# Three places for the rests of a masked sum, each behind one place of the block cycle, and idle matmuls counted by place

## The chip, the cores and the metric

The kernel runs on one core of a Trainium2 chip. The metric is the device time in microseconds (us). A core has engines that run side by side: TensorE (PE, matrix products), VectorE (DVE), ScalarE (ACT), GpSimd (POOL) and SyncE (SP, which here only issues transfers). Transfers between the main memory and the on-chip memory are done by 16 DMA engines, which take work from the queues of SP and ACT.

## What is computed

For each of 8 sequences, `x` is masked past `lengths`, summed cumulatively, and the sum at the midpoint is taken and multiplied with `w`:

```python
B, S, D = 8, 8192, 512
masked = x * (pos < lengths)
cs = np.cumsum(masked, axis=1)
mid_features = cs[b_idx, lengths // 2, :]
return np.matmul(mid_features[:, None, :], w).squeeze(1)
```

Only the first n = min(lengths // 2 + 1, lengths) rows of each sequence are needed, so each row of the result is the sum of n rows of `x`, times `w`. For the lengths drawn here n is 570, 2690, 256, 2057, 905, 3772, 3859 and 571: 30.1 MB of `x` of the 134 MB.

## The kernel before

Each sequence's n rows are cut into full blocks of 512 rows (1 MB, spread as 128 partitions x 4 rows) and a rest of fewer than 512 rows. Rows are summed by PE: a matmul with a one-hot column of weights (128 x 8) adds 128 rows into the row of the right sequence in `s_ps`. Four matmuls (in the records 8, each float matmul leaving two) do one block.

Blocks come in three kinds. The first blocks of sequences 0 and 1 are loaded at addresses known at build time into `first` (line 179). All further full blocks, 23 for these lengths, are "items" that go in pairs through a cycle of three places `xt[:, k]`, k = 0, 1, 2 (2 MB each). SP issues their loads (line 213) at addresses that DVE has computed. A round is one turn of the cycle, six blocks; the register `left` holds how many blocks are left, and `pairs` (line 146 on) does place k only if there are that many. One full block, of the last sequence, is loaded at the end in three parts into `last` (line 246), and its matmuls go straight to the transposed sum `t_ps`.

The rests are loaded by ACT in up to four parts of 256, 128, 64 and up to 64 rows (lines 276 and 288) into two places, `rem[:, q]`. A part that a rest doesn't have is skipped with a branch, and the semaphore is raised in its stead. The weights of a rest, `cur_rem[:, q]`, carry the mask; DVE copies them from `table`.

The order on each engine is written out by hand, and semaphores tie the engines together:

- PE, each round: while rests are left, wait for rest 0, use it, wait for rest 1, use it; then for each place k three idle matmuls (`keep_busy`, line 505; they use no data and keep the array busy), the wait for the pair, its matmuls. After all rounds a small matmul (line 509) tells DVE that the sum is complete.
- DVE, each round: the two copies of `cur_rem`, each after PE is done with that rest; then for each place the new weights `cur` (line 456), after PE is done with that pair. These writes free the places for ACT and SP.
- SP: per place, wait for it to be free, then issue one 2 MB load, or two or one of 1 MB. After the last round, the three loads of `last`.
- ACT: zero `rem` at the start (line 261, two instructions), then per rest wait for its place and issue its parts. This is a loop of four rounds of two.

After the loop DVE copies `s_ps` to `s_sb` in two halves, PE folds four partial sums of it into `t_ps` (line 498) between the parts of `last`, DVE transposes, PE multiplies with `w` (line 586), DVE and ACT copy the halves of the product, and two DMAs write it out.

Of the kernel before, what the change touches and what calls it, by code (L numbers as in the profile page):

```python
# [9 lines left out]
I32 = mybir.dt.int32  # L10
BF16 = mybir.dt.bfloat16
ALU = mybir.AluOpType
# [5 lines left out]
def kernel(  # L18
# [41 lines left out]
    PARTS = [(256, 0, 2, 4), (128, 1, 4, 4), (64, 3, 4, 2)]  # L60
    CUTS = [0, 2, 3, 4]
    WT = G * B
    xf = x.rearrange("b s d -> (b s) d")
    lens_words = lengths.tensor.reshape([B]).bitcast(I32).ap().rearrange("(o t) -> o t", o=1)

# [4 lines left out]
    def sb(name, shape, dt=F32):  # L70
        return ctx.enter_context(nc.sbuf_tensor(name, shape, dt))
# [4 lines left out]
    def sem(name):  # L76
        return tc.alloc_semaphore(name)
# [1 line left out]
    first = sb("first", [P, BLIND, G, D])  # L79
    xt = sb("xt", [P, NS, 2, G, D])  # L80
    last = sb("last", [P, G, D])
    rem = sb("rem", [P, 2, G, D])
    wt = sb("wt", [P, KC, D])
    lens1 = sb("lens1", [1, 2 * B], I32)
    len_f = sb("len_f", [1, B])
    len_i = sb("len_i", [P, B], I32)
    ones = sb("ones", [1, P])
# [31 lines left out]
    bits = sb("bits", [P, G], I32)  # L119
    thr_i = sb("thr_i", [P, 2], I32)  # L120
    thr = sb("thr", [P, G], I32)
    table = sb("table", [P, B * (WT + 1)])
    cur_rem = sb("cur_rem", [P, 2, WT])
    fold_i = sb("fold_i", [P, B], I32)
    fold = sb("fold", [P, B])
    s_sb = sb("s_sb", [P, D])
# [8 lines left out]


    s_done, s_free, s_full = [[sem(f"{n}{k}") for k in range(NS)] for n in ("done", "free", "full")]
    s_rdone, s_rfree, s_rem = [[sem(f"{n}{q}") for q in range(2)] for n in ("rdone", "rfree", "rem")]
    s_last = [sem(f"last{h}") for h in range(len(CUTS) - 1)]
    s_first = [sem(f"first{b}") for b in range(BLIND)]  # L140
    s_w, s_len1, s_out = sem("w"), sem("len1"), sem("out")
# [3 lines left out]

        eng.wait_ge(s, n).then_inc(s, -n)  # L146

    def pairs(eng, n, body, k=0):

        if k < NS:  # L150
            with eng.If_cmp(n, 2 * k + 1, "IS_GE"):
                body(k)
                pairs(eng, n, body, k + 1)

    def rounds_of(eng, n, least):

# [15 lines left out]
    DVE_LAST = DVE_ALL + 6  # L172
    PE_ALL, PE_SUM, PE_OUT = 2, 3, 4

    nc.sync.dma_start(out=lens1[:], in_=lens_words).then_inc(s_len1, 16)

    nc.scalar.dma_start(out=wt[:], in_=w.rearrange("(p kc) d -> p kc d", kc=KC)).then_inc(s_w, 16)
    for b in range(BLIND):
# [72 lines left out]
    @block.scalar  # L251
    def _(act):
        hint = act.mark_branch_hint_location()
        alu = act.reg_alu
        base, at, t = [act.alloc_register(f"act_{n}") for n in ("base", "at", "t")]
        words = [act.alloc_register(f"act_n{i}") for i in range(4)]
        pair, top = act.alloc_register("act_pair"), 2 * B - 4
        act.reg_mov(base, 0)
        act.reg_mov(pair, 0)
        for q in range(2):  # L260
            act.memzero(rem[:, q]).then_inc(s_rfree[q], 1)  # L261
        act.wait_ge(s_len1, 16)
        with act.Fori(0, B // 2):
            act.load(words, lens1[:, ds(act.snap(pair, min_val=0, max_val=top), 4)])
            for q in range(2):

                n = words[2 * q]
                alu(t, n, 1, ALU.logical_shift_right)
                alu(t, t, 1, ALU.add)
                alu(n, t, n, ALU.min)  # L270
                take(act, s_rfree[q], 1)
                for count, start, step, g in PARTS:
                    alu(t, n, count, ALU.bitwise_and)
                    with act.If_cmp(t, 1, "IS_GE"):
                        alu(t, n, ~(2 * count - 1), ALU.bitwise_and)
                        act.dma_start(
                            out=rem[start::step, q, :g],
                            in_=rows(act, at, base, t, count).rearrange("(p g) d -> p g d", g=g),
                        ).then_inc(s_rem[q], 16)
                    with act.Else():  # L280
                        act.sem_inc(s_rem[q], 16)
                alu(at, n, ~63, ALU.bitwise_and)
                alu(at, at, base, ALU.add)
                alu(t, n, 63, ALU.bitwise_and)

                def load_last(count):
                    to = rem[3::4, q, 2:] if count > 32 else rem[3:4 * count:4, q, 2:3]
                    act.dma_start(
                        out=to,
                        in_=xf[ds(act.snap(at), count)].rearrange("(g p) d -> p g d", g=to.shape[1]),  # L290
                    ).then_inc(s_rem[q], 16)

                with act.If_cmp(t, 33, "IS_GE"):
                    load_last(64)
                with act.Else():
                    with act.If_cmp(t, 17, "IS_GE"):
                        load_last(32)
                    with act.Else():
                        with act.If_cmp(t, 1, "IS_GE"):
                            load_last(16)  # L300
                        with act.Else():
                            act.sem_inc(s_rem[q], 16)
                alu(base, base, S, ALU.add)
            alu(pair, pair, 4, ALU.add)
            alu(pair, pair, top, ALU.min)

        with ending(act, "act_last", hint):
            act.wait_ge(s_pe, PE_OUT)
            for j in range(2):
                copy = act.copy(out=o_sb[1][:, j * P:(j + 1) * P], in_=o_ps[64 + 32 * j:64 + 32 * j + B, :P])  # L310
            copy.then_inc(s_act, 1)
            act.wait_ge(s_act, 1)
            act.dma_start(out=out[:, D // 2:], in_=o_sb[1][:]).then_inc(s_out, 16)
# [17 lines left out]
    def _(dve):  # L331
# [18 lines left out]
        step(dve.memset, step_c[:], float(S))  # L350
        step(dve.memset, step_c[:, BLIND - 1:BLIND], float(S - BLK))
        dve.wait_ge(s_len1, 16)
        step(dve.tensor_copy, out=len_f[:], in_=lens1[:, ::2])
        assert done == DVE_N, done

        def sinces(begin, a, b):
# [5 lines left out]
        def addresses(a, b):  # L362
# [5 lines left out]
            step(dve.tensor_tensor, out=addr[:, a:b], in0=item_a[:, a:b], in1=sum_a[:, a:b], op=ALU.add)  # L368

        dve.wait_ge(s_pool, 1)  # L370
        step(dve.tensor_tensor, out=above[:], in0=shape(lens1[:, ::2].unsqueeze(2), 1, B, K), in1=steps[:],
             op=ALU.is_ge)
        step(dve.tensor_reduce, out=usual1[:], in_=above[:], axis=mybir.AxisListType.X, op=ALU.add)
        step(dve.tensor_tensor_scan, out=begin1[:, 1:], data0=one8[:1], data1=usual1[:],
# [46 lines left out]
        step(dve.tensor_scalar, out=thr_i[:], in0=thr_i[:], scalar1=2, scalar2=None,  # L421
             op0=ALU.logical_shift_right)
        step(dve.tensor_tensor, out=thr[:, 2:], in0=thr_i[:], in1=shape(m4[:], P, 2), op=ALU.mult)
        tab = table[:].rearrange("p (b q) -> p b q", b=B)
        step(dve.tensor_tensor, out=cap[:], in0=shape(cnt[:].unsqueeze(2), P, B, G),
             in1=shape(bits[:].unsqueeze(1), P, B, G), op=ALU.bitwise_and)
        step(dve.tensor_tensor, out=tab[:, :, 0:G * B:B], in0=cap[:],
             in1=shape(thr[:].unsqueeze(1), P, B, G), op=ALU.is_gt)
        rests = table[:, :B * WT].rearrange("p (r q w) -> p r q w", q=2, w=WT)
        step(dve.tensor_copy, out=cur_rem[:], in_=rests[:, 0])  # L430
        assert done == DVE_MASK, done
        addresses(BLIND + PER, ITEMS)
# [9 lines left out]
        assert done == DVE_ALL, done  # L442
        dve.wait_ge(s_dve, done)

        left, at, of, rest_rounds = [dve.alloc_register(f"dve_{n}") for n in ("left", "at", "of", "rests")]
        dve.load([left], addr[:, 1:2])
        dve.reg_mov(at, BLIND + PER)
        dve.reg_mov(of, 1)
        dve.reg_mov(rest_rounds, B // 2 - 1)
        with dve.Fori(1, rounds_of(dve, left, B // 2)):  # L450
            less(dve, left, PER)

            def weights(k):
# [4 lines left out]
                    in1=since[:, 1:, here].rearrange("p b h -> p h b"), op=ALU.subtract,  # L458
                ).then_inc(s_free[k], 1)

            with dve.If_cmp(rest_rounds, 1, "IS_GE"):
                for q in range(2):
                    take(dve, s_rdone[q], 1)
                    dve.tensor_copy(  # L464
                        out=cur_rem[:, q],
                        in_=rests[:, ds(dve.snap(of, min_val=1, max_val=B // 2 - 1), 1), q].rearrange("p o w -> p (o w)"),
                    ).then_inc(s_rfree[q], 1)
            pairs(dve, left, weights)
            less(dve, rest_rounds, 1)
            dve.reg_alu(at, at, PER, ALU.add)  # L470
            dve.reg_alu(at, at, ITEMS - PER, ALU.min)
            dve.reg_alu(of, of, 1, ALU.add)
            dve.reg_alu(of, of, B // 2 - 1, ALU.min)

        dve.wait_ge(s_pe, PE_ALL)
        for h in range(2):
# [12 lines left out]
    def _(pe):  # L489
# [29 lines left out]
        pe.matmul(n_ps[:, :B], lhsT=ones[:], rhs=len_f[:], start=True, stop=True).then_inc(s_pe, 1)  # L519
        pe.wait_ge(s_pool, 2)  # L520
        keep_busy()
        left, rest_rounds, has_last = [pe.alloc_register(f"pe_{n}") for n in ("left", "rests", "has")]
        pe.wait_ge(s_dve, DVE_FIRST)
        pe.load([has_last, left], addr[:, :2])
        pe.reg_mov(rest_rounds, B // 2)
        rounds = rounds_of(pe, left, B // 2)
        for b in range(BLIND):
            keep_busy()
            pe.wait_ge(s_first[b], 16)
            for j in range(G):  # L530
                add(j, cur_first[:, b], first[:, b, j])
        keep_busy()
        pe.wait_ge(s_dve, DVE_MASK)
        with pe.Fori(0, rounds):
            with pe.If_cmp(rest_rounds, 1, "IS_GE"):
                for q in range(2):
                    take(pe, s_rem[q], 16 * (len(PARTS) + 1))
                    for j in range(G):
                        mm = add(j, cur_rem[:, q, j * B:(j + 1) * B], rem[:, q, j])
                    mm.then_inc(s_rdone[q], 1)  # L540

            def add_pair(k):
                keep_busy()
                take(pe, s_full[k], 32)
                with pe.If_cmp(left, 2 * k + 2, "IS_GE"):
                    for j in range(G):
                        add(j, cur[:, k, 1], xt[:, k, 1, j])
                for j in range(G):
                    mm = add(j, cur[:, k, 0], xt[:, k, 0, j])
                mm.then_inc(s_done[k], 1)  # L550

            pairs(pe, left, add_pair)
            less(pe, left, PER)
            less(pe, rest_rounds, 1)

        tell()

# [65 lines left out]
```

## Time and profile before

| | us |
|---|---|
| median of 14 runs | 84.86 |
| lowest, highest of them | 84.3, 88.84 |
| the profiled execution's own time | 84.59 |
| its span, from the first to the last record | 82.6 |
| PE busy in it | 56.1 (68%) |
| DVE busy | 15.2 (18%) |
| ACT busy | 5.5 (7%) |

The span is the part of the time that the profiler's records cover. Of the costlier groups (line, engine, operation, output from input, count; then busy time, mean ns of one; then idle time of the engine before them and what ended it):

```profile
L492 PE MATMUL s_ps<-xt,cur 128*8 128x512 f32 x184 | 26.5, 700 | 14.6 <-PEq L146 14.6
L505 PE MATMUL idle_ps<-idle 128*128 128x512 bf16 x44 | 14.8, 432 | 3.8 <-DVE since L340 3.6
L492 PE MATMUL s_ps<-rem,cur_rem 128*8 128x512 f32 x64 | 8.7, 636 | 2.4 <-PEq L146 2.4
...
L261 ACT ACTIVATE rem<-rem 128x2048 uint32<-128x2048 uint32 x2 | 3.7, 1900 | 0.0
```

"PEq L146" is the wait for a full place: PE's sequencer stands at line 146 until the semaphore of the load arrives. Four of the 48 idle matmuls have left no record of the matmul, only of its weight load. A mean of 700 ns for records that overlap says little of the pace; the timeline's stretches do.

### The profile page before, as it was taken

The numbers are of one execution on the slowest core, as the hardware profiler recorded it, in microseconds if no ns is written. First come the engines' busy times: TensorE is split into PE (matmuls) and PEld (weight loads), VectorE is DVE, ScalarE is ACT, GpSimd is POOL, SyncE is SP. The second block draws the span as 40 slices with busy tenths as digits, with TensorE's granted clock in tenths as the row PEclk, the third lists the DMA queues.
The fourth block names the chain that finished last, engine by engine and source line by source line (L and its number), as shares of the span: only waits on it lengthen the run. The fifth ranks groups of instructions, "written<-read, shape, count | busy, mean of one in ns | idle before, by whom it ended". The sixth has DMA issues, their size and how long they took to land. (4 is left out here: it accounts for less than half of the span.)

```text
span 82.6 us, 1482 instructions
## 1 busy us (share of the span) xinstructions
PE 56.1 (68%) x385; PEld 13.2 (16%) x389; DVE 15.2 (18%) x79; ACT 5.5 (7%) x6; POOL 1.6 (2%) x13
## 2 busy tenths in 40 slices
PE   2950699949991399985700993988408999399720
PEld 2300101102120122211100110211102122023510
DVE  2858888000000000100000000000000000001420
ACT  2991000000000000000000000000000000000020
POOL 5100000000000000000000000000000000000000
PEclk9999999999999857999999569999996599999999
DMA  2799999999999999999899999999999999899000
GB/s 32 285 436 420 476 421 423 391 470 404 428 404 436 397 420 404 432 432 468 381 444 385 456 428 397 460 432 389 431 407 466 428 404 468 373 406 376 3 9 7
DMA packets 3539, 31.26 MB, mean 378 GB/s; under 512 B 530, under 2 KB 546, under 8 KB 1202
## 3 DMA queue, kind: packets, MB, share of 16 engines
q1 hardware_dynamic: 2610, 27.27, 78.5%
q10 hardware_dynamic: 928, 3.97, 12.4%
q8 instruction: 1, 0.02, 0.1%
HBM read 31.23 MB, written 0.02 MB: 378 GB/s over the span
## 5 line engine op out<-in xcount | busy, mean ns | idle before, releaser
L492 PE MATMUL s_ps<-xt,cur 128*8 128x512 f32 x184 | 26.5, 700 | 14.6 <-PEq L146 14.6
L505 PE MATMUL idle_ps<-idle 128*128 128x512 bf16 x44 | 14.8, 432 | 3.8 <-DVE since L340 3.6
L492 PE MATMUL s_ps<-rem,cur_rem 128*8 128x512 f32 x64 | 8.7, 636 | 2.4 <-PEq L146 2.4
L456 DVE TENSOR_TENSOR cur<-since 128x16 f32 x9 | 1.7, 186 | 40.0 <-DVEq L146 40.0
L492 PEld LDWEIGHTS s_ps<-xt,cur 128*8 128x8 f32 x184 | 4.4, 94 | 28.6 <-issue 28.6
L505 PEld LDWEIGHTS idle_ps<-idle 128*128 128x128 bf16 x48 | 3.6, 102 | 20.4 <-issue 18.8
L310 ACT COPY o_sb<-o_ps 8x128 f32<-8x128 f32 x2 | 0.5, 260 | 72.7 <-PE o_ps L586 72.7
L261 ACT ACTIVATE rem<-rem 128x2048 uint32<-128x2048 uint32 x2 | 3.7, 1900 | 0.0
L492 PEld LDWEIGHTS s_ps<-rem,cur_rem 128*8 128x8 f32 x64 | 2.0, 106 | 10.4 <-issue 10.4
L492 PE MATMUL s_ps<-first,cur_first 128*8 128x512 f32 x16 | 3.6, 984 | 0.0
L516 PE MATMUL s_ps<-zero 1*128 1x512 f32 x2 | 2.1, 1137 | 1.6 <-DVE zero L340 1.6
L464 DVE COPY cur_rem<-table 128x32 f32 x6 | 1.1, 181 | 8.9 <-DVEq L146 8.9
L340 DVE COPY s_sb<-s_ps 128x256 f32<-128x256 f32 x2 | 0.9, 426 | 9.8 <-PE idle_ps L509 9.8
L498 PE MATMUL t_ps<-last,e_last 128*8 128x128 f32 x32 | 1.7, 273 | 0.0
L261 ACT ACT_TABLE_LOAD x1 | 1.3, 1283 | 1.4 <-PEq L607 1.4
L586 PE MATMUL o_ps<-wt,t_sb 128*8 128x128 f32 x32 | 1.1, 273 | 0.4 <-DVE t_sb L340 0.4
L340 DVE TENSOR_TENSOR part_a<-since,step_a 1x42 f32<-1x42 f32 (+1 forms) x2 | 1.1, 564 | 0.1
L586 PEld LDWEIGHTS o_ps<-wt,t_sb 128*8 128x8 f32 x32 | 0.8, 89 | 0.7 <-issue 0.7
L498 PEld LDWEIGHTS t_ps<-last,e_last 128*8 128x8 f32 x32 | 0.8, 89 | 0.4 <-issue 0.3
L498 PE MATMUL t_ps<-s_sb,fold 128*8 128x128 f32 x8 | 0.8, 274 | 0.1
L340 DVE TENSOR_TENSOR since<-item,begin 1x42 f32<-1x42 int32 (+1 forms) x2 | 0.8, 422 | 0.1
L519 PEld LDWEIGHTS n_ps<-len_f,ones 1*128 1x128 f32 x2 | 0.7, 333 | 1.0 <-DVE len_f L340 0.5
(66 smaller groups left out, 13.3 us busy)
## 6 DMA issues: line engine op xcount, KB each, us to landing
xt<-in_x_dram SPq DMA_DIRECT2D x10, 2048.0 KB, 12.5
xt<-in_x_dram SPq DMA_DIRECT2D x3, 1024.0 KB, 9.8
first<-in_x_dram SPq DMA_DIRECT2D x2, 1024.0 KB, 7.9
rem<-in_x_dram ACTq DMA_DIRECT2D x3, 512.0 KB, 8.8
wt<-in_w_dram ACTq DMA_DIRECT2D x1, 1024.0 KB, 4.8
rem<-in_x_dram ACTq DMA_DIRECT2D x3, 256.0 KB, 8.8
last<-in_x_dram SPq DMA_DIRECT2D x1, 512.0 KB, 6.3
last<-in_x_dram SPq DMA_DIRECT2D x2, 256.0 KB, 6.5
```

The source lines that it names most:

```text
L261: act.memzero(rem[:, q]).then_inc(s_rfree[q], 1)
L310: copy = act.copy(out=o_sb[1][:, j * P:(j + 1) * P], in_=o_ps[64 + 32 * j:64 + 32 * j + B, :P])
L340: do(*args, **kw).then_inc(s_dve, 1)
L456: dve.tensor_tensor(out=cur[:, k], in0=since[:, :B, here].rearrange("p b h -> p h b"), in1=since[:, 1:, here].rearrange("p b h -> p h b"), ...
L464: dve.tensor_copy(out=cur_rem[:, q], in_=rests[:, ds(dve.snap(of, min_val=1, max_val=B // 2 - 1), 1), q].rearrange("p o w -> p (o w)"),).t ...
L492: return pe.matmul(s_ps[32 * j:32 * j + B], lhsT=weights, rhs=rows, start=False, stop=False, skip_group_check=True, tile_position=(0, 32 * j))
L498: return pe.matmul(t_ps[32 * j:32 * j + B, :P], lhsT=weights, rhs=row[:, P * j:P * (j + 1)], start=False, stop=False, skip_group_check=Tru ...
L505: pe.matmul(idle_ps[:], lhsT=idle[:, :P], rhs=idle[:], start=True, stop=True)
L516: pe.matmul(s_ps[:], lhsT=zero[:], rhs=zero[:, :1].to_broadcast((1, D)), start=True, stop=False, skip_group_check=True)
L519: pe.matmul(n_ps[:, :B], lhsT=ones[:], rhs=len_f[:], start=True, stop=True).then_inc(s_pe, 1)
L586: mm = pe.matmul(o_ps[32 * j:32 * j + B, :P], lhsT=t_sb[:, kc, :B], rhs=wt[:, kc, j * P:(j + 1) * P], start=(kc == 0), stop=(kc == KC - 1) ...
```

## The change

The rests get three places instead of two, `rem[:, q]` and `cur_rem[:, q]` with q = 0, 1, 2, and take RR = 3 rounds (3, 3 and 2) instead of four. On PE and DVE the rest q no longer stands at the head of the round but behind place k = q of the cycle. ACT's loop takes three rests a turn, with a count `some` of those that are left, and reads six words of lengths at a time; two further words of `lens1` are zeroed for that, and a third memzero clears the new place. The idle matmuls ahead of a wait are 10 for place 0, 4 for place 1, none for place 2, and 4 for place 2 where the round is full; 2 more stand ahead of rest 0; the 3 ahead of the loop go. The wait for a pair stands inside the two branches on `left` instead of ahead of them.

```diff
-    rem = sb("rem", [P, 2, G, D])
+    rem = sb("rem", [P, NS, G, D])
...
-    def pairs(eng, n, body, k=0):
+    def pairs(eng, n, body, k=0, most=NS):
-        if k < NS:
+        if k < most:
             with eng.If_cmp(n, 2 * k + 1, "IS_GE"):
                 body(k)
-                pairs(eng, n, body, k + 1)
+                pairs(eng, n, body, k + 1, most)
...
# ACT
-        for q in range(2):
+        act.reg_mov(some, B)
+        act.memzero(lens1[:, 2 * B:])
+        for q in range(NS):
             act.memzero(rem[:, q]).then_inc(s_rfree[q], 1)
         act.wait_ge(s_len1, 16)
-        with act.Fori(0, B // 2):
-            act.load(words, lens1[:, ds(act.snap(pair, min_val=0, max_val=top), 4)])
-            for q in range(2):
+        with act.Fori(0, RR):
+            act.load(words, lens1[:, ds(act.snap(pair, min_val=0, max_val=top), 2 * NS)])
+            def rest(q):
...
+            for q in range(NS):
+                if q < B - NS * (RR - 1):
+                    rest(q)
+                else:
+                    with act.If_cmp(some, q + 1, "IS_GE"):
+                        rest(q)
+            less(act, some, NS)
...
# DVE
-            with dve.If_cmp(rest_rounds, 1, "IS_GE"):
-                for q in range(2):
-                    take(dve, s_rdone[q], 1)
+            for k in range(NS):
+                pairs(dve, left, weights, k, k + 1)
+                with dve.If_cmp(some, k + 1, "IS_GE"):
+                    take(dve, s_rdone[k], 1)
                     dve.tensor_copy(
...
-            pairs(dve, left, weights)
...
# PE
-        keep_busy()
+        BUSY = [10, 4, 0]
         pe.wait_ge(s_dve, DVE_MASK)
         with pe.Fori(0, rounds):
-            with pe.If_cmp(rest_rounds, 1, "IS_GE"):
-                for q in range(2):
-                    take(pe, s_rem[q], 16 * (len(PARTS) + 1))
-                    for j in range(G):
-                        mm = add(j, cur_rem[:, q, j * B:(j + 1) * B], rem[:, q, j])
-                    mm.then_inc(s_rdone[q], 1)
-
             def add_pair(k):
-                keep_busy()
-                take(pe, s_full[k], 32)
-                with pe.If_cmp(left, 2 * k + 2, "IS_GE"):
+                def second():
+                    take(pe, s_full[k], 32)
                     for j in range(G):
                         add(j, cur[:, k, 1], xt[:, k, 1, j])
+
+                keep_busy(BUSY[k])
+                with pe.If_cmp(left, 2 * k + 2, "IS_GE"):
+                    if k == NS - 1:
+                        keep_busy(4)
+                    second()
+                with pe.Else():
+                    take(pe, s_full[k], 32)
                 for j in range(G):
                     mm = add(j, cur[:, k, 0], xt[:, k, 0, j])
                 mm.then_inc(s_done[k], 1)
 
-            pairs(pe, left, add_pair)
+            for k in range(NS):
+                pairs(pe, left, add_pair, k, k + 1)
+                with pe.If_cmp(some, k + 1, "IS_GE"):
+                    if k == 0:
+                        keep_busy(2)
+                    take(pe, s_rem[k], 16 * (len(PARTS) + 1))
+                    for j in range(G):
+                        mm = add(j, cur_rem[:, k, j * B:(j + 1) * B], rem[:, k, j])
+                    mm.then_inc(s_rdone[k], 1)
```

More of the change, by code (lines that the diff above doesn't have):

```diff
@@ L62 @@
     WT = G * B
+    RR = -(-B // NS)
     xf = x.rearrange("b s d -> (b s) d")
@@ L81 @@
     last = sb("last", [P, G, D])
-    rem = sb("rem", [P, 2, G, D])
+    rem = sb("rem", [P, NS, G, D])
     wt = sb("wt", [P, KC, D])
-    lens1 = sb("lens1", [1, 2 * B], I32)
+    lens1 = sb("lens1", [1, 2 * NS * RR], I32)
     len_f = sb("len_f", [1, B])
@@ L121 @@
     thr = sb("thr", [P, G], I32)
-    table = sb("table", [P, B * (WT + 1)])
-    cur_rem = sb("cur_rem", [P, 2, WT])
+    table = sb("table", [P, max(B * (WT + 1), NS * RR * WT)])
+    cur_rem = sb("cur_rem", [P, NS, WT])
     fold_i = sb("fold_i", [P, B], I32)
@@ L137 @@
     s_done, s_free, s_full = [[sem(f"{n}{k}") for k in range(NS)] for n in ("done", "free", "full")]
-    s_rdone, s_rfree, s_rem = [[sem(f"{n}{q}") for q in range(2)] for n in ("rdone", "rfree", "rem")]
+    s_rdone, s_rfree, s_rem = [[sem(f"{n}{q}") for q in range(NS)] for n in ("rdone", "rfree", "rem")]
     s_last = [sem(f"last{h}") for h in range(len(CUTS) - 1)]
@@ L173 @@
     PE_ALL, PE_SUM, PE_OUT = 2, 3, 4
-    nc.sync.dma_start(out=lens1[:], in_=lens_words).then_inc(s_len1, 16)
+    nc.sync.dma_start(out=lens1[:, :2 * B], in_=lens_words).then_inc(s_len1, 16)
     nc.scalar.dma_start(out=wt[:], in_=w.rearrange("(p kc) d -> p kc d", kc=KC)).then_inc(s_w, 16)
@@ L255, in _ @@
         base, at, t = [act.alloc_register(f"act_{n}") for n in ("base", "at", "t")]
-        words = [act.alloc_register(f"act_n{i}") for i in range(4)]
-        pair, top = act.alloc_register("act_pair"), 2 * B - 4
+        words = [act.alloc_register(f"act_n{i}") for i in range(2 * NS)]
+        pair, top = act.alloc_register("act_pair"), 2 * NS * (RR - 1)
+        some = act.alloc_register("act_some")
         act.reg_mov(base, 0)
         act.reg_mov(pair, 0)
-        for q in range(2):
+        act.reg_mov(some, B)
+        act.memzero(lens1[:, 2 * B:])
+        for q in range(NS):
             act.memzero(rem[:, q]).then_inc(s_rfree[q], 1)
         act.wait_ge(s_len1, 16)
-        with act.Fori(0, B // 2):
-            act.load(words, lens1[:, ds(act.snap(pair, min_val=0, max_val=top), 4)])
-            for q in range(2):
+        with act.Fori(0, RR):
+            act.load(words, lens1[:, ds(act.snap(pair, min_val=0, max_val=top), 2 * NS)])
+            def rest(q):
                 n = words[2 * q]
@@ L303, in _ @@
                 alu(base, base, S, ALU.add)
-            alu(pair, pair, 4, ALU.add)
+            for q in range(NS):
[5 more added lines that the diff above has]
+            less(act, some, NS)
+            alu(pair, pair, 2 * NS, ALU.add)
             alu(pair, pair, top, ALU.min)
@@ L352, in _ @@
         dve.wait_ge(s_len1, 16)
-        step(dve.tensor_copy, out=len_f[:], in_=lens1[:, ::2])
+        step(dve.tensor_copy, out=len_f[:], in_=lens1[:, :2 * B:2])
         assert done == DVE_N, done
@@ L370, in _ @@
         dve.wait_ge(s_pool, 1)
-        step(dve.tensor_tensor, out=above[:], in0=shape(lens1[:, ::2].unsqueeze(2), 1, B, K), in1=steps[:],
+        step(dve.tensor_tensor, out=above[:], in0=shape(lens1[:, :2 * B:2].unsqueeze(2), 1, B, K), in1=steps[:],
              op=ALU.is_ge)
@@ L423, in _ @@
         step(dve.tensor_tensor, out=thr[:, 2:], in0=thr_i[:], in1=shape(m4[:], P, 2), op=ALU.mult)
-        tab = table[:].rearrange("p (b q) -> p b q", b=B)
+        tab = table[:, :B * (WT + 1)].rearrange("p (b q) -> p b q", b=B)
         step(dve.tensor_tensor, out=cap[:], in0=shape(cnt[:].unsqueeze(2), P, B, G),
@@ L428, in _ @@
              in1=shape(thr[:].unsqueeze(1), P, B, G), op=ALU.is_gt)
-        rests = table[:, :B * WT].rearrange("p (r q w) -> p r q w", q=2, w=WT)
+        rests = table[:, :NS * RR * WT].rearrange("p (r q w) -> p r q w", q=NS, w=WT)
         step(dve.tensor_copy, out=cur_rem[:], in_=rests[:, 0])
@@ L443, in _ @@
         dve.wait_ge(s_dve, done)
-        left, at, of, rest_rounds = [dve.alloc_register(f"dve_{n}") for n in ("left", "at", "of", "rests")]
+        left, at, of, some = [dve.alloc_register(f"dve_{n}") for n in ("left", "at", "of", "some")]
         dve.load([left], addr[:, 1:2])
@@ L448, in _ @@
         dve.reg_mov(of, 1)
-        dve.reg_mov(rest_rounds, B // 2 - 1)
-        with dve.Fori(1, rounds_of(dve, left, B // 2)):
+        dve.reg_mov(some, B - NS)
+        with dve.Fori(1, rounds_of(dve, left, RR)):
             less(dve, left, PER)
@@ L459, in weights @@
                 ).then_inc(s_free[k], 1)
-            with dve.If_cmp(rest_rounds, 1, "IS_GE"):
-                for q in range(2):
-                    take(dve, s_rdone[q], 1)
+            for k in range(NS):
+                pairs(dve, left, weights, k, k + 1)
+                with dve.If_cmp(some, k + 1, "IS_GE"):
+                    take(dve, s_rdone[k], 1)
                     dve.tensor_copy(
-                        out=cur_rem[:, q],
-                        in_=rests[:, ds(dve.snap(of, min_val=1, max_val=B // 2 - 1), 1), q].rearrange("p o w -> p (o w)"),
-                    ).then_inc(s_rfree[q], 1)
-            pairs(dve, left, weights)
-            less(dve, rest_rounds, 1)
+                        out=cur_rem[:, k],
+                        in_=rests[:, ds(dve.snap(of, min_val=1, max_val=RR - 1), 1), k].rearrange("p o w -> p (o w)"),
+                    ).then_inc(s_rfree[k], 1)
+            less(dve, some, NS)
             dve.reg_alu(at, at, PER, ALU.add)
@@ L472, in _ @@
             dve.reg_alu(of, of, 1, ALU.add)
-            dve.reg_alu(of, of, B // 2 - 1, ALU.min)
+            dve.reg_alu(of, of, RR - 1, ALU.min)
         dve.wait_ge(s_pe, PE_ALL)
@@ L521, in _ @@
         keep_busy()
-        left, rest_rounds, has_last = [pe.alloc_register(f"pe_{n}") for n in ("left", "rests", "has")]
+        left, some, has_last = [pe.alloc_register(f"pe_{n}") for n in ("left", "some", "has")]
         pe.wait_ge(s_dve, DVE_FIRST)
         pe.load([has_last, left], addr[:, :2])
-        pe.reg_mov(rest_rounds, B // 2)
-        rounds = rounds_of(pe, left, B // 2)
+        pe.reg_mov(some, B)
+        rounds = rounds_of(pe, left, RR)
         for b in range(BLIND):
@@ L550, in add_pair @@
                 mm.then_inc(s_done[k], 1)
-            pairs(pe, left, add_pair)
+            for k in range(NS):
[7 more added lines that the diff above has]
+                    mm.then_inc(s_rdone[k], 1)
             less(pe, left, PER)
-            less(pe, rest_rounds, 1)
+            less(pe, some, NS)
         tell()
```

## The prediction

> **What bounds the kernel now.** I read the page's slices first, then the windows of equal rate, then the landings and the timeline of the end.
>
> ```profile
> DMA  2799999999999999999899999999999999899000
> GB/s 32 285 436 420 476 421 423 391 470 404 428 404 436 397 420 404 432 432 468 381 444 385 456 428 397 460 432 389 431 407 466 428 404 468 373 406 376 3 9 7
> ...
> HBM read 31.23 MB, written 0.02 MB: 378 GB/s over the span
> ```
>
> The DMA engines are full from slice 3 to slice 37, and in the last three slices nearly nothing moves. Windows that cover the full part show one rate (columns: window, its length, busy time and count of PE, PEld, DVE, ACT, POOL, then clock, DMA share, GB/s):
>
> ```profile
> 3.00:14.80 11.80, 8.17 (x28) 1.42 (x26) 9.32 (x50) 3.53 (x2) 0.00 (x0) 1.00 1.01 428
> 14.80:25.00 10.20, 9.01 (x63) 1.78 (x60) 0.74 (x4) 0.00 (x0) 0.00 (x0) 1.00 1.01 426
> ...
> 65.00:74.00 9.00, 7.59 (x57) 1.54 (x50) 0.19 (x1) 0.00 (x0) 0.00 (x0) 0.94 0.99 419
> ```
>
> Share about 1 in each, 419 to 428 GB/s. From 3.0 to 76.5 us 31.1 MB move, which is 423 GB/s. So the transfers bind, not the matmuls: PE is busy 68% and starts a pair only when its data has landed. What follows the last byte is the rest of the time. The last transfer and the end of PE's work on it:
>
> ```profile
> L246 SPq DMA_DIRECT2D last<-in_x_dram x1: 333/333/333, 70.5 to 70.5; - x1
> ...
> DMA to landing us min/median/max: 6.6/6.6/6.6
> ...
> 77.01 0.28 PE L498 MATMUL t_ps<-s_sb,fold 128*8 128x128 f32 x2
> ...
> 77.09 0.28 PE L498 MATMUL t_ps<-last,e_last 128*8 128x128 f32 x2
> ```
>
> Issue at 70.5 and 6.6 us: the last quarter of `last` lands at about 77.05, and its matmuls begin at 77.09. The fold ahead of them began at 77.01, after the second DVE copy of s_sb. So two things arrive together here, the last bytes and the chain from PE's last pair through DVE. From 77.05 to the span's end are 5.55 us of product, copy and output DMA.
>
> Is there slack between PE and the queue? A view of `xt` on the DMA queue, window by window, gives issue and landing:
>
> ```profile
> L213 SPq DMA_DIRECT2D xt<-in_x_dram x1: 340/340/340, 22.8 to 22.8; - x1
> ...
> DMA to landing us min/median/max: 10.1/10.1/10.1
> ```
>
> The pair issued at 22.8 lands at 32.9; the pair ahead of it (place 2, on which PE waits until 28.23) was issued at 10.6, took 17.3 and lands at 27.9. At 22.8 the queue thus still had 27.9 - 22.8 = 5.1 us of work. The same sum over all later issues of `xt` gives 5.0 to 7.7 us. A place may be freed 5 us later than now before a DMA engine runs dry.
>
> [...] pairs with no rest between land 4.9 to 5.0 us apart (27.9, 32.9, 37.9), which is 2.10 MB / 423 GB/s. [...] the clock is 0.50 from 28.46 to 31.87, 45.52 to 48.94 and 62.58 to 65.99, each 3.41 us, each behind a window in which PE was busy 0.21 to 0.26 us:
>
> ```profile
> 59.17:62.58 3.41, 0.26 (x4) 0.13 (x8) 0.00 (x0) 0.00 (x0) 0.00 (x0) 1.00 1.02 426
> 62.58:65.99 3.41, 3.41 (x20) 0.77 (x16) 0.00 (x0) 0.00 (x0) 0.00 (x0) 0.50 1.06 452
> ...
> 69.40:72.82 3.42, 2.06 (x19) 0.39 (x15) 0.00 (x0) 0.00 (x0) 0.00 (x0) 1.00 0.99 417
> ```
>
> A window with 2.06 us busy kept the full clock. In the cold stages the DMA share stays at 1.06.
>
> **The change part by part.** For these lengths there are 23 full blocks (184 matmul records of `xt`, 8 a block), so four rounds before and after: 6, 6, 6 and 5 blocks. Bytes are the same: 27.27 and 3.97 MB on the two queues.
>
> *Idle matmuls.* Before, 12 ahead of the loop and 4 x 9 inside, 48 (the count of their weight loads). After: 9 ahead; a round of 6 blocks has 10 + 2 + 4 + 0 + 4 = 20; the last has 10 + 4 + 0 = 14. Sum 9 + 60 + 14 = 83, so 35 more at 0.25 us (three take 0.75 us from start to start) are 8.75 us of PE. They lie where PE waited: its waits before matmuls of `xt` and `rem` are 14.6 + 2.4 us. PE's path from the end of place 2 to the start of place 0 was two rests and three idles, 2 x 1.04 + 0.75 = 2.83 us; it becomes one rest and ten idles, 1.04 + 2.5 = 3.54 us: 0.7 us later at most. From place 0 to place 1: 0.75 us becomes 0.5 + 1.04 + 1.0 = 2.54 us, 1.8 us more. From 1 to 2: 0.75 becomes 1.04 + 1.0 = 2.04 us, 1.3 more. Even if all three added up in one round, 3.8 us, the 5.0 us of queued work covers it. And place 2, where the clock stays full, takes 1.90 us instead of 3.43 cold. Cost of the idles at nothing; without that cover each would cost its 0.25 us on the transfers.
>
> *The first round's rests.* Before, rests 0 and 1 came ahead of place 0, which PE started at 19.76. After, place 0 starts at 15.10 + 2.5 = 17.6 (its data landed at 6.4 + 10.3 = 16.7), ends at 19.5, and its next load goes out about 2.3 us earlier. An earlier issue into a full queue brings nothing.
>
> *A third memzero on ACT.* 1.9 us more, and a two-word one ahead, for which I estimate 0.2 us: rest 0 is issued at about 8.8 instead of 6.68 and, with the 8.0 us that it took before, lands at 16.8. PE wants it at 20.0. Rest 1: last transfer 11.19 + 2.1 + 6.7 = 20.0, wanted at about 23.9. Rest 2 (one 512 KB transfer, issued some 2 us later, 9.2 us) lands at about 25, wanted behind place 2 at 30. None late. In later rounds a rest has a whole cycle (about 17 us, 27.9 to 44.9) from the freeing of its place; issuing took up to 3.5 us (freed 19.56, issued 23.07, with three parts skipped) and landing at most 10.2: 13.7 us. Covered, by 3 us.
>
> *DVE.* Copies and weights alternate instead of two copies ahead. Weights of place 1 now wait behind the copy that waits for rest 0 to be used; PE does that rest ahead of place 1, so it is done. The table is 288 instead of 264 wide and the first copy 96 instead of 64: under 0.1 us, beside 1.5 us of waiting for the first pair. SP's queue is untouched; its three loads and `last` follow the freeing of places.
>
> *The wait inside the branch.* The wait for a pair now stands behind the branch on `left`. Before, a landing at 27.9 was followed by matmuls at 28.23; the wait for `last`, with no branch behind it, took under 0.1 us (69.42 + 6.3 = 75.7 to 75.79). So up to 0.3 us for each pair, hidden as long as transfers bind.
>
> *The end.* Last round: place 1 lands at 72.0 (59.2 + 12.8), place 2's single block at 66.9 + 7.6 = 74.5. Before, its matmuls began at 74.92 behind three idles; after, none stand ahead: start 74.5, 0.4 us earlier. The s_sb copies move by that, the folds too. Then `last` is alone in front: its final matmuls start at 77.1 as now; the fold's four records are no longer in between, so they end some 0.07 us earlier. That is all the gain I find: 77.64 becomes 77.57.
>
> Sum against the profiled execution: span 82.6 - 0.07, time 84.59 - 0.07 = 84.52 us. That execution lies 0.27 us under the median of the 14 runs, 84.86; for a median I add it back: 84.8 us.
>
> **Rivals.** *Slower, the clock at the end.* In the last round no rest stands behind place 0 any more. If place 0 is done at 69.0 and four idles end at 70.0, PE waits 2.0 us for the 72.0 landing (1.36 us before). Should the clock fall then, place 1 takes 3.43 instead of 1.90 us and ends at 75.4; the single block ends at about 76.7, its copies (0.9 us) at 77.65, the fold and last matmuls at about 78.3 instead of 77.6: 85.5 us as a median. It decides if a window with some 40% busy is idle enough; 8% was, 60% wasn't. [...] For it: the waits at the end lengthen; against: a gap of 2.0 us leaves 1.4 us busy in any window of 3.41.
>
> *Slower, a rest arrives late.* If skipped parts on ACT and a 10 us landing add up to more than a cycle, PE waits with three pairs landed, and after 5 us the queue runs dry. A rest 6 us late would cost 1 us: 85.8. The 3 us of cover speak against it.
>
> *Faster, the rate.* By windows of 10 us the rate ran from 415 to 433 GB/s. If evenly spread rests and earlier issues keep it 1% higher, 73.5 us of transfers shorten by 0.7 us: 84.1. For it: the queue is deeper at the first issue; against: windows without any rest in flight (65 to 74, 419 GB/s) are no faster than those with.
>
> *The change does nothing at all*: the same bytes, rate and tail, 84.86. This lies within the forecast.
>
> **How the numbers follow.** A measurement of this kernel tells 0.5% (0.42 us) from no change. Forecast, same within that, 0.60, with a range of its own of 84.5 to 85.2; the rate rival 0.20; the clock at the end 0.12; a late rest 0.08. So faster 0.20, same 0.60, slower 0.20. Before's undisturbed runs spread over 84.3 to 85.6, and that noise goes on top; 84.1 to 85.6 takes in the rate and the clock cases and leaves out late rests beyond that.
>
> **What would show it.** Idle matmuls 83; `last` lands within 0.5 us of 77.0 and the DMA digits stay 9 to slice 36; no 0.50 clock, or only where the share stays 1; the final matmuls directly behind the last landing. The forecast is wrong if the DMA share drops under 0.9 for a microsecond before 74, if PE's wait for `rem` shows up before an `xt` that has landed for over 5 us, or if the clock is 0.50 after 70.

## The result, and the profile after

The changed kernel takes 86.12 us (median of 10 runs, 85.50 to 86.74), the kernel before 84.73 us in the same measurement: ratio 1.0169, 95% interval 1.0134 to 1.0203. It is slower by 1.4 us, and outside the range of the prediction. Ratios and intervals here leave out disturbed executions and are not the quotients of the medians beside them.

The profiled execution took 86.17 us with a span of 84.4 us; before, 84.59 and 82.6. The slices of the changed kernel:

```profile
PEclk9999999999999999999999999999999999965999
DMA  3799999999999899999999999999999999992000
GB/s 51 284 423 423 435 419 444 458 381 474 388 482 404 373 435 416 411 406 459 421 408 462 404 404 431 454 396 466 404 451 419 427 435 388 406 397 75 0 0 8
```

The DMA engines are as full as before, to slice 36, and the clock is full up to slice 35, which it wasn't before; but it falls in the slices of the end. The three falls in mid-kernel are gone and a new one has come where it matters. The end itself, in the views of the last load and of PE's timeline:

```profile
L247 SPq DMA_DIRECT2D last<-in_x_dram x1: 333/333/333, 70.2 to 70.2; - x1
...
DMA to landing us min/median/max: 8.0/8.0/8.0
```

```profile
73.33 4.39 PE L503 MATMUL s_ps<-xt,cur 128*8 128x512 f32 x24 [2.02 <-PEq L147]
...
78.75 0.28 PE L509 MATMUL t_ps<-s_sb,fold 128*8 128x128 f32 x2
78.76 0.28 PE L509 MATMUL t_ps<-last,e_last 128*8 128x128 f32 x2
...
78.87 0.48 PE L509 MATMUL t_ps<-last,e_last 128*8 128x128 f32 x6
```

The last part of `last` was issued at 70.2, 0.3 us earlier than before, and landed at 78.2, some 1.15 us later than before (77.05). Its first matmuls began 0.55 us after that, at 78.76, because the second fold, which stands ahead of them and waits for the copies of s_sb, was late (78.75). So the loss of this execution has two parts: 1.15 us in the transfers, and 0.5 us more between the last landing and the last matmuls (0.55 us, against 0.04 before). Together they are 1.7 of the 1.8 us by which the span grew.

The transfers were late in a peculiar way. Windows of the DMA engines at the end (columns: window, length, busy time and count of PE, PEld, DVE, ACT, POOL, then clock, DMA share, GB/s):

```profile
76.00:76.40 0.40, 0.40 (x4) 0.00 (x0) 0.00 (x0) 0.00 (x0) 0.00 (x0) 0.50 0.64 231
76.40:76.60 0.20, 0.20 (x4) 0.00 (x0) 0.00 (x0) 0.00 (x0) 0.00 (x0) 0.50 0.06 21
76.60:77.00 0.40, 0.40 (x8) 0.13 (x2) 0.00 (x0) 0.00 (x0) 0.00 (x0) 0.50 0.07 26
77.00:77.40 0.40, 0.40 (x4) 0.10 (x3) 0.00 (x0) 0.00 (x0) 0.00 (x0) 0.50 0.07 26
77.40:77.80 0.40, 0.40 (x13) 0.26 (x9) 0.00 (x0) 0.00 (x0) 0.00 (x0) 0.50 0.05 20
```

The same stretch before:

```profile
76.40:76.60 0.20, 0.06 (x6) 0.05 (x8) 0.17 (x2) 0.00 (x0) 0.00 (x0) 1.00 0.25 82
76.60:77.00 0.40, 0.40 (x12) 0.26 (x12) 0.36 (x1) 0.00 (x0) 0.00 (x0) 1.00 0.00 0
```

From 76.4 to 77.8 us the share is 0.05 to 0.07, and 1/16 is 0.0625. So by the share fifteen engines have finished, at about the time at which all of them did before (76.6), and one works alone for 1.4 us. (The trace gives the share, not the engines' numbers.) A view of the DMA queues between 32 and 34 us shows something that stood elsewhere before:

```profile
q8 instruction: 1, 0.02, 3.3%
```

This is one packet of a queue that the trace calls "instruction": by that name, a read of the program itself. Its record has 16,384 bytes (16 KB here). The share is 3.3% of 16 engines in 2 us, so it occupied one engine for 1.06 us. Before, the same single read stands between 79 and 82.6 us, after the last load:

```profile
q8 instruction: 1, 0.02, 2.0%
```

The page lists it either way, with 0.02 MB and no time. Whose queue q8 is, the trace doesn't say, nor whether the engine of this read is the one that is late at the end; the times agree (1.06 us and 1.15 us). Whether such a read costs time was to be tested: the kernels below with one in mid-stream take 1.1% to 1.7% longer.

### The profile page after: what moved, and what is told of

It reads as the page before. It is cut to its first block, busy times and chain, and to the rows that moved or that the text cites. A ratio compares the mean times of both kernels' runs of the same rounds, so it can differ in the third digit from the quotient of the medians.

```text
span 84.4 us, 1582 instructions
## 1 busy us (share of the span) xinstructions
PE 59.4 (70%) x421; PEld 16.3 (19%) x424; DVE 15.1 (18%) x78; ACT 7.4 (9%) x8; POOL 1.6 (2%) x13
## 3 DMA queue, kind: packets, MB, share of 16 engines
q1 hardware_dynamic: 2610, 27.27, 76.7%
q10 hardware_dynamic: 928, 3.97, 12.4%
## 5 line engine op out<-in xcount | busy, mean ns | idle before, releaser
L503 PE MATMUL s_ps<-xt,cur 128*8 128x512 f32 x184 | 23.3, 622 | 15.3 <-PEq L147 15.2
L516 PE MATMUL idle_ps<-idle 128*128 128x512 bf16 x80 | 22.0, 407 | 4.1 <-DVE since L351 3.6
L516 PEld LDWEIGHTS idle_ps<-idle 128*128 128x128 bf16 x83 | 6.9, 100 | 24.5 <-issue 19.1
L321 ACT COPY o_sb<-o_ps 8x128 f32<-8x128 f32 x2 | 0.5, 258 | 72.5 <-PE o_ps L605 72.4
L265 ACT ACTIVATE rem<-rem 128x2048 uint32<-128x2048 uint32 x3 | 5.5, 1892 | 0.0
L503 PE MATMUL s_ps<-first,cur_first 128*8 128x512 f32 x16 | 2.9, 818 | 0.0
L503 PEld LDWEIGHTS s_ps<-rem,cur_rem 128*8 128x8 f32 x64 | 1.5, 89 | 4.4 <-issue 4.4
L527 PEld LDWEIGHTS s_ps<-zero 1*128 1x128 f32 x2 | 0.5, 304 | 1.6 <-DVE zero L351 1.6
```

The lines of the kernel that those rows point to most:

```text
L503: return pe.matmul(s_ps[32 * j:32 * j + B], lhsT=weights, rhs=rows, start=False, stop=False, skip_group_check=True, tile_position=(0, 32 * j))
L516: pe.matmul(idle_ps[:], lhsT=idle[:, :P], rhs=idle[:], start=True, stop=True)
L527: pe.matmul(s_ps[:], lhsT=zero[:], rhs=zero[:, :1].to_broadcast((1, D)), start=True, stop=False, skip_group_check=True)
```

## The experiments

Theory A: the change makes an engine's program longer, 16 KB of instructions are then read while `x` streams, one DMA engine falls behind by about the time of that read, and every later transfer ends with it. The fall of the clock in the last round comes on top. Theory B: the new order of rests and the idle matmuls cost the time themselves. PE's program is counted from the source, in the same way for all kernels below (a float matmul as four instructions, two loads of weights and two matmuls as in the records; an idle one as two): 418 instructions before, 463 after. No trace shows this count, and each kernel was traced in one execution.

### Filler that never runs, engine by engine

In the kernel before, instructions behind a branch that is never taken, at the end of the loop of one engine.

```diff
+            with act.If_cmp(base, 1 << 20, "IS_GE"):
+                for _ in range(50):
+                    alu(t, t, 0, ALU.add)
```

> The kernel before, with 50 register additions that never run behind a branch at the end of ACT's loop, about as many instructions as the change adds to ACT. Theory A (the change makes some engine's program longer, so that a 16 KB block of instructions is read while the transfers of x run; it occupies one of the 16 DMA engines for 1.1 us, and from then on every transfer ends with that engine): if ACT is the engine, the read moves from 80.1 us to mid-stream, the last landing from 77.05 to about 78.2, and the time goes up by 1.0 us, ratio 1.012. Theory B (idle matmuls, order of rests and the clock at the end cost the time): ratio 1.000.

Measured: ratio 1.0007 (0.9973 to 1.0041). No read of 16 KB stands in its trace, in mid-stream or behind the last load (one that shows as 0.00 MB stands at its start).

```diff
+            with dve.If_cmp(rest_rounds, 1000, "IS_GE"):
+                for _ in range(8):
+                    dve.reg_alu(of, of, 0, ALU.add)
```

> The kernel before, with 8 register additions that never run behind a branch at the end of DVE's loop (the change makes DVE's program 5 to 9 instructions longer, and the first turn of DVE's loop ends at about the time of the read). Theory A with DVE as the engine: the read of instructions in mid-stream, last landing about 78.2, ratio 1.012. Theory B: 1.000.

Measured: ratio 0.9999 (0.9969 to 1.0030), again no read. The last landing is at 70.0 + 7.4 = 77.4 here, 0.3 us later than before without any read, so not every such lag is that of a read. In these two kernels PE's program is that of before, and yet the read that before has at 80 us is missing: what makes it come at its time isn't settled by PE's length alone.

```diff
+            with pe.If_cmp(rest_rounds, 1000, "IS_GE"):
+                keep_busy(20)
```

> The kernel before, with 20 idle matmuls (40 instructions) that never run behind a branch at the end of PE's loop, about as many as the change adds to PE. Theory A with PE as the engine: read in mid-stream, last landing about 78.2, ratio 1.012. Theory B: 1.000.

Measured: ratio 1.0106 (1.0017 to 1.0194), 85.99 us, median of four. The views of the DMA queues from 32 to 34 us, and of the end:

```profile
q8 instruction: 1, 0.02, 2.9%
```

```profile
77.20:77.60 0.40, 0.40 (x13) 0.15 (x9) 0.00 (x0) 0.00 (x0) 0.00 (x0) 1.00 0.08 31
77.60:78.00 0.40, 0.40 (x21) 0.29 (x16) 0.16 (x1) 0.00 (x0) 0.00 (x0) 1.00 0.07 26
```

The same read and, from 77.2 us on, the same lone engine at the end (before that, from 76.4 us, the shares were 0.33 and 0.17), with no rest moved and no idle matmul added to those that run; the last landing is at 72.5 + 6.2 = 78.7. So 40 instructions more on PE brought the read, where 50 on ACT and 8 on DVE brought none.

### Where the filler stands, and how much

The 40 instructions put into the branch behind the loop that these lengths never take:

```diff
         with pe.Else():
+            keep_busy(20)
             fold_half(0)
```

> The kernel before, with the 20 idle matmuls (40 instructions) that never run put behind the loop, into the branch for a last sequence without a full block, instead of at the loop's end. If the length of PE's whole program decides when the next 16 KB are read: read at about 32 us as with the filler in the loop, last landing about 78.2 to 78.7, ratio 1.011. If the place of the loop's end decides: the read stays at 80, ratio 1.000.

Measured: ratio 1.0160 (1.0115 to 1.0205), last landing 72.0 + 6.3 = 78.3. The read is there, but between 42 and 44 us, ten later than expected. So 40 instructions more on PE brought it in both places, inside the loop and behind it. What decides when it comes stays open: with the filler at the loop's end the times differ too, 32 to 34 us above and 25 to 27 in the next run.

> The kernel before, with 13 idle matmuls (26 instructions) that never run at the end of PE's loop, instead of 20. By a count of the programs' PE instructions that reads 418 for before, 425 for the shortened changed kernel, 460 and 463 for the two with the read in mid-stream, this one has 446. [...] no read in mid-stream, ratio 1.000. If the edge is lower: ratio 1.011, read at about 32 us.

Measured: ratio 1.0149 (1.0104 to 1.0194). One read between 25 and 27 us. So a count of 446 brings the read; the forecast of none was the author's estimate and rested on no run.

```diff
+            with pe.If_cmp(rest_rounds, 1000, "IS_GE"):
+                keep_busy(300)
```

> The kernel before with 600 instructions on PE that never run, instead of 40. Theory A: more than one block of 16 KB [...] is read while the transfers run; if all go over the same DMA engine, each adds about 1.1 us to the last landing, which comes at 79 to 81 and the ratio is 1.025 to 1.045; if PE's jump over the filler waits for its block, PE may stand still for some us more, which the queued 5 us cover. If the number of reads doesn't matter: 1.011 as with 40. Theory B: 1.000.

Measured: 88.32 us, median of four, without an interval. There are five reads between 25 and 60 us, and the last landing is at 79.9, 2.8 us later than before, not five times 1.1. But this run doesn't measure the price of a read: ahead of the rests of two rounds PE also stood still for 3.50 and 5.35 us (1.24 at most in the kernel before), places came free late, and the engines were no longer full, as this window shows:

```profile
45.00:50.00 5.00, 2.86 (x23) 0.55 (x19) 0.37 (x2) 0.00 (x0) 0.00 (x0) 1.00 0.87 358
```

It is inconclusive on how reads add up.

### The change with a shorter PE program

Cut out of the changed kernel, with the cycle of places as it is but for two idle matmuls. Without the last branch this kernel, and the two built on it below, leave out the folding for a last sequence without a full block, so that they serve only for lengths like these:

```diff
         pe.wait_ge(s_pool, 2)
-        keep_busy()
...
         for b in range(BLIND):
-            keep_busy()
             pe.wait_ge(s_first[b], 16)
...
-                    if k == 0:
-                        keep_busy(2)
...
-        with pe.Else():
-            fold_half(0)
-            fold_half(1).then_inc(s_pe, 1)
```

> The changed kernel with PE's program cut by 38 instructions, all outside the cycle of places but two idle matmuls: the idle matmuls ahead of the first blocks, the two ahead of rest 0, and the branch for a last sequence without a full block, which these lengths never take. It is then 7 instructions longer than before's instead of 45. Theory A (a longer PE program has its next 16 KB read in mid-stream, which holds back one DMA engine): no read before the outputs, last landing back at 77.0, and what is left is the fall of the clock at the end, in about half of the executions: median ratio 1.000 to 1.006. Theory B (rests behind the places and idles cost the time): ratio stays at 1.017, last landing at 78.2.

Measured: ratio 1.0009 (0.9981 to 1.0036). No read in mid-stream, last landing 77.0. The loss is gone with the rests in their new places. The 20 executions fall into 11 of 84.2 to 84.6 us and nine of 84.9 to 85.6. The profiled one took 84.88 and shows what delayed it, in windows of one clock stage:

```profile
69.88:73.29 3.41, 1.39 (x13) 0.38 (x16) 0.00 (x0) 0.00 (x0) 0.00 (x0) 1.00 1.00 420
73.29:76.70 3.41, 3.36 (x29) 0.76 (x25) 0.18 (x1) 0.00 (x0) 0.00 (x0) 0.50 0.89 344
```

PE was busy 1.39 of 3.41 us, 41%, and the next stage ran at half clock, across the last pair. Whether the other eight were late for the same reason wasn't traced.

### The clock at the end

The same kernel with 7 idle matmuls ahead of places 0 and 1 each, `BUSY = [7, 7, 0]`:

> The same with 7 and 7 idle matmuls ahead of places 0 and 1 instead of 10 and 4: the same number of instructions, and the wait ahead of the last round's second pair shortens from 2.0 to about 1.3 us. Theory A with the clock at the end as the second part: ratio 1.000, no clock of one half after 70 us. Theory B: 1.010 or more.

Measured: ratio 1.0006 (0.9980 to 1.0032), no half clock at the end (from 67 us on 16 matmuls of a pair take 1.90 us), 15 of 20 executions within 84.4 to 84.8. The ratio is that of the kernel above, so this pair shows no gain. Five executions still took 85.1 to 85.8 us, two of them (85.18 and 85.09) at a mean clock of 1.00: a late execution needs no fall of the clock.

The changed kernel at full length with `BUSY = [10, 12, 0]`:

> The changed kernel with 12 idle matmuls ahead of place 1 instead of 4, so that PE has no wait of 2 us ahead of the last round's second pair. If the fall of the clock at the end costs the 0.6 us that the changed kernel's profile shows between last landing and last matmuls, the runs lose their upper half: median 85.6 instead of 86.1, ratio to before 1.011. The read of instructions in mid-stream stays (theory A). Under theory B alone, with the clock as the whole loss, the ratio is 1.000.

Measured: ratio 1.0127 (1.0102 to 1.0153), the read between 25 and 27 us, last landing 71.5 + 6.7 = 78.2, full clock at the end. Of 20 executions 14 are within 85.4 to 85.8 and six at 86.3 to 87.1, where the changed kernel had five of ten above 86.4; the intervals of the two ratios overlap. The read's share stays.

How busy PE was ahead of a fall can be read from the traces. Two windows of the changed kernel's, each with the one behind it:

```profile
20.02:23.43 3.41, 1.55 (x16) 0.53 (x15) 0.18 (x1) 0.00 (x0) 0.00 (x0) 1.00 1.02 432
23.43:26.85 3.42, 3.23 (x28) 0.75 (x20) 0.37 (x2) 0.00 (x0) 0.00 (x0) 1.00 0.93 398
...
71.22:74.63 3.41, 1.39 (x15) 0.38 (x16) 0.00 (x0) 0.00 (x0) 0.00 (x0) 1.00 0.99 410
74.63:78.04 3.41, 3.28 (x29) 0.81 (x25) 0.23 (x1) 0.00 (x0) 0.00 (x0) 0.50 0.51 193
```

With 45% busy the clock stayed, with 41% it fell. If the traces of the kernel before (from 14.8 us on) and of the changed one (from 13.2 us on, where the clock records begin) are cut into stages of 3.41 us that begin and end where their clock changes, 35 stages at full clock result: behind the four with 7%, 7%, 8% and 41% busy the clock fell, behind the 31 with 45% to 100% it stayed. Between 41% and 45% these traces show nothing.

### One part of the change alone

Its idle matmuls and the wait inside the branches, in the kernel before:

> The idle matmuls and the wait inside the branches alone, as the change has them, in the kernel before, with its two places for rests at the head of the round. PE's count is 440, 22 more than before; 7 more gave no read in mid-stream and 26 more gave one. If the edge lies under 22 more: read in mid-stream, last landing about 78.2, ratio 1.013. If above: ratio 1.000, with some executions later by the clock at the end. Theory B with the idles as the cost, whatever is read: slower without a read in mid-stream.

Measured: ratio 1.0148 (1.0095 to 1.0201), one read between 25 and 27 us, last landing 70.1 + 8.2 = 78.3. PE waited 0.3 us for that landing, so its own work wasn't late.

Its rests behind the places, with three idle matmuls everywhere:

> The rests behind the places alone: the changed kernel with before's idle matmuls, three ahead of each place and three ahead of the loop. PE's count is 447, 29 more than before, above the edge (26 more gave a read). Theory A: read in mid-stream, last landing about 78.2, ratio 1.013 to 1.016. Theory B with the idles as the cost: 1.000.

Measured: ratio 1.0174 (1.0110 to 1.0238), one read between 31 and 34 us, last landing 78.2. Each half alone adds enough instructions to PE: 22 and 29. Here too PE waited for the last landing, 0.2 us, and the ratio is no smaller than that of the whole change, so the ratios don't separate a share of the clock from the read's.

The late landing stands in all seven traces with a read in mid-stream whose time was compared with before: the last part of `last` lands between 78.2 and 78.7 us in them, at 77.05 before, and by 77.4 in the five others (the fifth of them comes next).

### A version ahead of both

The shortened kernel with 7 idle matmuls ahead of place 1 and 2 ahead of place 2 in a full round:

```diff
-        BUSY = [10, 4, 0]
+        BUSY = [10, 7, 0]
...
                     if k == NS - 1:
-                        keep_busy(4)
+                        keep_busy(2)
```

> The shortened changed kernel with 7 idle matmuls ahead of place 1 instead of 4, and 2 instead of 4 ahead of place 2: the wait ahead of the last round's second pair falls from 2.0 to 1.3 us and the clock stays full there. Theory A: no read in mid-stream, no executions at 84.9 and above but the disturbed ones, median 84.3 to 84.5, ratio 0.998 to 1.000; it can't be much faster than before, since the transfers bind. Theory B: 1.010 or more.

Measured: 84.32 us, ratio 0.9973 (0.9958 to 0.9989), all 22 executions within 84.24 to 84.44. Its end:

```profile
72.12 1.90 PE L503 MATMUL s_ps<-xt,cur 128*8 128x512 f32 x16 [1.38 <-PEq L147]
74.61 1.05 PE L503 MATMUL s_ps<-xt,cur 128*8 128x512 f32 x8 [0.59 <-PEq L147]
...
77.10 0.41 PE L509 MATMUL t_ps<-last,e_last 128*8 128x128 f32 x8
```

The last block waits for its data only, and the final matmuls start with the landing (69.0 + 8.1 = 77.1) and end at 77.51, where the prediction had 77.57. The gain is small, as the prediction's sum said of the change: 0.1 us by the medians (84.44 before), 0.2 by the ratio. The late group of the first shortened kernel, nine of 20, is gone; this pair is the clearest sign that the half clock at the end had a part in it.

## Why the prediction was wrong

*What bounds the kernel*: right. The DMA share is about 1 up to the end in both, and 1.15 us of the loss are in the transfers.

*"Bytes are the same: 27.27 and 3.97 MB on the two queues"*, and with it *"Cost of the idles at nothing"*: here it failed. The two queues of loads did stay the same, but there is a third, and its 0.02 MB moved from behind the last load into the stream. The step costed 35 more idle matmuls by their 0.25 us on PE and asked what covers that; it put the 45 more instructions of PE's program at nothing without a reason. Their cost ran through a resource with no cover, a single DMA engine. It was also wrong to take the 16 engines for one pipe of 423 GB/s. At the end fifteen were done by 76.5 us, and the last transfer landed at 78.2, when the sixteenth was: with 16 KB read by one engine in mid-stream it came 1.15 us later, where by an estimate an even spread would have cost 0.04 us (16.4 KB / 423 GB/s).

*The cover of the idle matmuls*: right. 83 weight loads, and with the same cycle but for two idle matmuls and a shorter program the ratio is 1.0009. The queued 5 us did cover PE's later starts. The range of that sum was misread: the landings and issues before give 5.1 to 9.5 us (for the issue at 41.2, 50.7 - 41.2), not 5.0 to 7.7; the argument needs only the lower end.

*The rests*: none came late; PE has no idle time ahead of `rem` in the changed kernel (2.4 us before). The third memzero was mis-costed: I expected rest 0 to be issued at about 8.8, and it went out at 6.85, since ACT waits for the clearing of that one place alone. It had no effect.

*The rate*: not higher. Windows up to 74 us move 419 to 429 GB/s in the changed kernel, 415 to 433 before. The earlier issue brought nothing: place 0's second load went out at 19.7 instead of 22.8 us and landed at 34.7 instead of 32.9.

*The end*: right in mechanism, 0.1 us, seen in the last experiment; in the changed kernel itself it was covered by the two losses. Two of the prediction's own signs came: the last landing was more than 0.5 us from 77.0, and the clock was 0.50 after 70 us.

*The rival on the clock*: its mechanism came true in the profiled execution. The wait was 2.02 us (2.0 forecast) and the window 1.39 us busy (1.4 forecast); that was held for probably enough, with a chance of 0.12 for the rival, and it wasn't. Its price was 0.5 us between landing and matmuls, where 0.7 was forecast. Not shown is how often it comes. The changed kernel's ten runs are five of 85.5 to 85.8 and five of 86.4 to 86.7 us, but these groups lie 0.9 us apart, only one execution was traced, and other kernels have late executions without a fall.

Sum: the read alone gives 1.15 us and, if the clock fell in half of the executions, it would add 0.25 to 0.3 us, against 1.4 measured. That these agree is in part luck: the share of half is assumed, and kernels with the read in which PE waited for the last landings lose as much (ratios 1.0127, 1.0148 and 1.0174). What triggers the read at just that time (between 25 and 44 us) remains open, as does whether two reads cost twice.

## What to carry to other kernels

A kernel that is bound by transfers can pay for instructions too, this one 1.1% to 1.7% of its time: look in the list of DMA queues for the program's own reads, and at what time they stand, before and after a change that only adds code. Code that never runs counted here as well (ratio 1.0106 with 40 instructions of it). When a stream is full and its end is late by about a microsecond, look for a DMA share of one sixteenth at the end (0.05 to 0.07 here). And idle matmuls that keep the clock have a second price, two instructions each: 7 ahead of the last round's second pair kept it in the traces here where 4 didn't, and the kernel had room for them only after other code of PE's had gone.

## What the runs showed of the hardware

- One read of 16 KB of instructions occupied one DMA engine for 0.9 to 1.1 us; with it in mid-stream the last landing came 1.1 to 1.7 us later than before. Seven kernels with such a read took 1.1% to 1.7% longer, and five without took 0.997 to 1.001 of before.
- The edge for PE here lies between a count of 427 (the last experiment's kernel, no read in mid-stream) and 440.
- In the traces of the kernel before and of the changed one, the four stages of 3.41 us at full clock with 7% to 41% busy were followed by half clock, and the 31 with 45% to 100% were not. In the first shortened kernel one with 41% was.
